# A sparse gate table built by indirect DMA adds in place of one-hot matrix products

## The chip, the cores and the metric

The kernel runs on one core of a Trainium2 chip. That core has five engines with one in-order instruction queue each: TensorE (PE, with PEld for its weight loads), VectorE (DVE), ScalarE (ACT), GpSimd (POOL) and SyncE (SP). SP, ACT and POOL can issue DMA transfers, which 16 shared DMA engines carry out. The metric is the time of one execution in microseconds (us) on the device; lower is better. The kernel before takes 4821.69 us, the median of three runs (4821.6 to 4826.84).

## What is computed

One transformer layer on 512 tokens of width 2048 in float32: a mixer (mLSTM and forgetting attention), a cross attention to a memory of 256 rows, and a PEER feed-forward, each with a residual and a layer norm. The change lies in the last:

```python
def peer_ffn(x, w_pq, sub_keys, expert_u, expert_v):
    q = (x @ w_pq).reshape(B, S, PEER_HEADS, 2, PEER_DK // 2)
    sc = einsum('bshpd,hpnd->bshpn', q, sub_keys)
    top_s, top_i = lax.top_k(sc, 16)                        # on each of two sides, of 128 keys
    cand_s = top_s[..., 0, :, None] + top_s[..., 1, None, :]    # 16 x 16 candidates
    cand_i = top_i[..., 0, :, None] * 128 + top_i[..., 1, None, :]
    best_s, best_pos = lax.top_k(cand_s, 16)
    idx = take_along_axis(cand_i, best_pos)                 # 8 heads x 16 experts a token
    g = softmax(best_s)
    a = einsum('tkd,td->tk', expert_u[idx], x)
    hact = gelu(a) * g
    return einsum('tk,tkd->td', hact, expert_v[idx])
```

There are 128 x 128 = 16,384 experts. Each token picks 16 in each of 8 heads. Two heads of a token may pick the same expert; their gates then add up.

## The kernel before

All large products are run as three float32r products, of a high and a low part of each operand. Weights come in 512 KB pieces on SP's queue (`load_raw`). For each, ACT makes the high part `whi` (line 133) and DVE the low part `wlo` (line 134, a tensor_tensor of two SBUF inputs); this pair is called the split. `work["last"]` holds the last split, and `after(i, other)` makes instruction `i` wait for another; it paces work that is put in between.

The tokens are cut into four blocks of 128. Block 0 (path A) runs ahead of the other three (path B). Early in the kernel, block 0's merge and tail are woven with block B's mLSTM heads (`weave`, line 1127).

The PEER part treats tokens in two ways. 232 of them, block 0 and the last 104 of block 3, are *gathered*: for each of a token's picks, POOL issues an indirect DMA (`gather_rows`, line 917) that fetches 128 expert rows of 8 KB, one a partition, into the three-deep buffer `rows`. DVE then makes the dot product (line 947), or adds the row (line 950). The other `NDENSE = 280` tokens (blocks 1, 2 and 24 tokens of block 3) are *dense*: every expert is computed for them, and a gate table, zero almost everywhere, picks out the few that count.

The dense part has two stages. `stage_a(c)` takes one chunk of 128 experts: 48 matmuls, then a gelu on ACT into `ga` (line 1307). The first `LOOK = 88` chunks run ahead and store `ga` to HBM (`gad`). Then `stage_o` runs in 16 blocks of eight chunks. For each chunk `stage_h` loads the gates `G` (line 1318, four chunks at a time) and `ga`, multiplies them (line 1324) and splits them into `hph` and `hpl`; the matmuls into `po` follow. The remaining 40 chunks of `stage_a` run within these blocks. The rows of the gathered tokens of block 3, as `jobs`, are spread over both stages, `EARLY = 66` of them in the first.

The gates come from `topk` (lines 1218 to 1244): for each block, `select` finds `i0`, `i1` (the two key numbers) and `g` (the score) of the 128 picks of each token, and `soften` makes gates of the scores. `rows_of` copies block 3's picks on POOL into `eid` and `egg` for the gathers. Then, in the code before, the table is built by products. The three arrays are transposed. For each dense token, DVE makes two one-hot rows, one of `i0` and one of `i1` (line 1269), ACT scales one with the gate (line 1274), and PE multiplies them (line 1275); summed over the 128 picks, this gives the token's 128 x 128 gates. ACT copies them from PSUM into `stage` (line 1278) and sends them to HBM as `gd` (line 1280).

The code is written in one order, but a scheduler decides how the instructions of different parts follow each other on each engine; so the build of the table lies among the chunks of `stage_a`. On POOL, each DMA takes one of eight completion semaphores in turn and waits until the last transfer with that semaphore has landed.

Of the kernel before, what the change touches and what calls it, by code (L numbers as in the profile page):

```python
# [21 lines left out]
P = 128  # L22
# [8 lines left out]
PH, PKEYS, TOPK = 8, 128, 16  # L31
NDENSE = 280
GATHERED = ((64, 64), (32, 32), (24, 8))
GB = 56
NEG = -1.0e30
ALPHA = 2.0 ** 0.25
EPS = 1e-5
# [8 lines left out]
def build(tc, I, out):  # L46
    nc = tc.nc
    with ExitStack() as ctx:
# [25 lines left out]
        def nm(s):  # L74
            cnt[0] += 1
            return f"{s}_{cnt[0]}"
# [50 lines left out]
        ioti = cp.tile([P, P], I32, tag="ioti", name="ioti")  # L127
        nc.gpsimd.iota(ioti, pattern=[[1, P]], base=0, channel_multiplier=0)
        nc.vector.tensor_copy(iota, ioti)


        def split(hi, lo, src):
# [583 lines left out]
        def merge(R, Y, G, cpair, tmp):  # L716

            for g in range(4):
                def ev_b(s, b, g=g):
                    m1, t = tmp(R.n), tmp(R.n)  # L720
                    nc.gpsimd.dma_start(m1, mg[g * 4 + s, :, R.cols])
                    nc.gpsimd.dma_start(t, sgd[g * 4 + s, :, R.cols])
                    nc.vector.tensor_mul(t, t, b[:, :R.n])
                    nc.vector.tensor_add(t, t, m1)
                    G.append(cpair())
                    split(*G[-1], t)

                yield from R.group(I["w_br_fx"][g], Y, ev_b)
# [138 lines left out]
        def soften(tp, g):  # L867

            e = g.rearrange("p (h k) -> p h k", k=16)
            sm = tp.tile([P, 8], F32, tag="sm", bufs=2, name=nm("s"))  # L870
            nc.scalar.activation(e, e, AF.Exp)
            nc.vector.tensor_reduce(out=sm, in_=e, axis=AX.X, op=ALU.add)
            nc.vector.reciprocal(sm, sm)
            nc.vector.tensor_tensor(e, e, sm.unsqueeze(2).to_broadcast([P, 8, 16]), op=ALU.mult)
# [153 lines left out]
        with tc.tile_pool(name="sa", bufs=1, side="right", reuse_waits="tile") as sa:  # L1028
# [95 lines left out]
            mbs = ctx.enter_context(ExitStack())  # L1124
            mb = mbs.enter_context(tc.tile_pool(name="mb", bufs=1, reuse_waits="tile"))
            heads = mlstm(B, mb, dict(ka=2, pre=3, qk=5, v=5, o=3, nM=1, pt=5), hold_d)
            weave(chain(merge(A, YA, GA, ac, at), tail_a()), heads, 0.36)

        gat = ctx.enter_context(tc.tile_pool(name="gat", bufs=1, side="right", reuse_waits="tile"))
        work.update(jobs=gathered(0, 0, P, 0, lambda: work["last"], 2), rate=258 / 305)  # L1130
# [45 lines left out]
        with tc.tile_pool(name="xb", bufs=1, reuse_waits="tile") as xp:  # L1176
# [6 lines left out]
            class Rows(list):  # L1183
# [20 lines left out]


        NC_ = PKEYS
        gd = dp.tile([P, NDENSE // GB, NC_, GB], F32, tag="gd", name="gd")
        gap = ctx.enter_context(tc.tile_pool(name="gap", bufs=1, reuse_waits="tile"))
        E = weights(ctx, "w2", 3, 3, 3)
        gad = dp.tile([NC_, P, NDENSE], F32, tag="gad", name="gad")  # L1210
# [3 lines left out]

        sel = {t: {n: pp.tile([P, P], F32, tag=f"{n}{t}", name=f"sel_{n}{t}") for n in ("i0", "i1", "g")}
               for t in range(1, TB)}

        with tc.tile_pool(name="topk", bufs=1, reuse_waits="tile") as tp:
            scs, QB = {}, []
            for g in query(B, X2, lambda: tp.tile([P, B.n], F32, tag="qT", bufs=6, name=nm("qT")), QB):  # L1220
                if g is None:
                    continue
                g, = g
                keysT = tp.tile([P, 4, P], F32, tag="keysT", bufs=2, name=nm("keysT"))
                nc.sync.dma_start(keysT, I["keysT"][:, 4 * g:4 * g + 4])
                for t in range(TB - 1, 0, -1):
                    bank = sm_bank()
                    for j in range(4):
                        nc.tensor.matmul(bank[:, j * P:(j + 1) * P], QB[g][j][:, (t - 1) * P:t * P],
                                         keysT[:, j, :], start=True, stop=True)  # L1230
                    first = t == TB - 1
                    scs[t, g] = tp.tile([P, 512], F32, tag=f"sc{first}", bufs=2 if first else 8, name=nm("sc"))
                    nc.scalar.copy(scs[t, g], bank)
                    if t == TB - 1:
                        select(tp, sel[t], 2 * g, scs[t, g])
            while work["jobs"] is not None:
                if next(work["jobs"], None) is None:
                    work["jobs"] = None
            soften(tp, sel[TB - 1]["g"])
            rows_of(tp, sel[TB - 1], [(1 + i, r0, n) for i, (r0, n) in enumerate(GATHERED)])  # L1240
            for t in range(1, TB - 1):
                for g in range(4):
                    select(tp, sel[t], 2 * g, scs[t, g])
                soften(tp, sel[t]["g"])

        def o_bank(i=0):
            return BK["pool"].tile([P, 512], F32, tag="mm", bufs=BK["mm"], name=nm("po"))


        gs = ExitStack()  # L1250
        gp = gs.enter_context(tc.tile_pool(name="gbuild", bufs=1, reuse_waits="tile"))
        selT = {n: gp.tile([P, NDENSE], F32, tag=n + "T", name=n + "T") for n in ("i0", "i1", "g")}
        turned = 0
        for hb in range(NDENSE // GB):
            while turned * P < (hb + 1) * GB:
                bank = o_bank()
                n = min(P, NDENSE - turned * P)
                for j, m in enumerate(("i0", "i1", "g")):
                    nc.tensor.transpose(bank[:, j * P:(j + 1) * P], sel[turned + 1][m], ident)
                for j, m in enumerate(("i0", "i1", "g")):  # L1260
                    nc.vector.tensor_copy(selT[m][:, turned * P:turned * P + n], bank[:, j * P:j * P + n])
                turned += 1
            stage = [gp.tile([P, 32, GB], F32, tag="stage", bufs=5, name=nm("stage")) for _ in range(4)]
            for q in range(GB // 4):
                ta = hb * GB + q * 4
                bank = o_bank()
                o0, o1 = (gp.tile([P, 4, P], F32, tag=f"o{k}", bufs=2, name=nm("o")) for k in (0, 1))
                for o, k in ((o0, "i0"), (o1, "i1")):
                    onehot = nc.vector.tensor_tensor(o, iota.unsqueeze(1).to_broadcast([P, 4, P]),
                                                     selT[k][:, ta:ta + 4].unsqueeze(2).to_broadcast([P, 4, P]),  # L1270
                                                     op=ALU.is_equal)
                for u in range(4):
                    c = slice(ta + u, ta + u + 1)
                    nc.scalar.activation(o0[:, u], o0[:, u], AF.Copy, scale=selT["g"][:, c])
                    nc.tensor.matmul(bank[:, u * P:(u + 1) * P], o1[:, u], o0[:, u], start=True, stop=True)
                bv = bank.rearrange("p (t c) -> p c t", t=4)
                for ch in range(4):
                    nc.scalar.copy(stage[ch][:, :, q * 4:q * 4 + 4], bv[:, ch * 32:ch * 32 + 32])
            for ch in range(4):
                nc.scalar.dma_start(gd[:, hb, ch * 32:ch * 32 + 32], stage[ch])  # L1280
        gs.close()
        pre.close()


        mn = ctx.enter_context(tc.tile_pool(name="main", bufs=1, reuse_waits="tile"))
        acc = mn.tile([P, NK, NDENSE], F32, tag="acc", name="acc")

        J = 8
        LOOK = 88
        EARLY = 66  # L1290
        fetched, hs, gates = {}, {}, {}

        rings[:] = [W, E]
# [19 lines left out]
        def stage_h(c):  # L1313

            for f in range(c, min(c + 3, NC_)):
                if f // 4 not in gates:
                    gates[f // 4] = mn.tile([P, NDENSE // GB, 4, GB], F32, tag="G", bufs=2, name=nm("G"))
                    nc.sync.dma_start(gates[f // 4], gd[:, :, f:f + 4])
# [4 lines left out]
            gv = ga.rearrange("p (b t) -> p b t", t=GB)  # L1323
            nc.vector.tensor_mul(gv, gv, gates[c // 4][:, :, c % 4])
            a, b = pair(mn, "hp", [P, NDENSE], 2 * J + 2)
            split(a, b, ga)
            hs[c] = (a, b)
# [137 lines left out]
                    last_rows(0, NT, rest)  # L1465

        njobs, done = sum(2 * n + 1 + REST for _, n in GATHERED), 0
        for a in range(LOOK):
            if a >= LOOK - J:
                work["tie"] = onehot  # L1470
            stage_a(a)
            while done * LOOK < a * EARLY:
                next(jobs, None)
                done += 1
        work["tie"] = None


        room = [4 if c0 < LOOK - J else 10 for c0 in range(0, NC_ - 2 * J, J) for _ in range(2 * J)]
# [91 lines left out]
```

## Time and profile before

The profiled execution took 4818.19 us; its span, from the first instruction to the last, is 4816.5 us.

| what | value |
|---|---|
| median of the runs | 4821.69 us |
| profiled execution, its span | 4818.19 us, 4816.5 us |
| busy share of PE, DVE, ACT, POOL | 97%, 78%, 46%, 21% |
| bytes moved | 1437 MB, 298 GB/s in the mean |
| granted clock of TensorE | 0.986 |
| first chunk of stage_a begins | 3056 us |
| one-hot rows, first and last | 3391.6, 3621.7 us |
| first output product | 3676.8 us |

A busy PE is not PE at its peak, as matmuls are pipelined. In rows of busy time by stage, each engine has its busy microseconds and, in brackets, its instructions; behind them stand the granted clock, the share of the DMA engines and GB/s. In a timeline, a row has its start, its length, and in square brackets the idle time before it and what ended it. A POOL row of a DMA is the time to issue it, not the transfer. A row of DMA issues ends with the median time to landing.

### The profile page before, as it was taken

To read this page: it belongs to the slowest core of one execution; us is meant where nothing else is said; L and a number is where in the kernel's file an instruction comes from. 1 tells how busy PE (TensorE), PEld (TensorE's weight loads), DVE (VectorE), ACT (ScalarE), POOL (GpSimd) and SP (SyncE) were. 2 spreads that over 40 slices of the span, in tenths; PEclk is the share of its full clock that TensorE was granted. 3 is DMA by queue.
4 is the path that set the end of the run, shared out by engine and by line. 5 is a ranking of instruction groups with operands and counts; after the bars stand their busy time and mean duration, and the time that the engine had idled before them with its cause. 6 is when DMAs were issued, how large, how long until landed. Compare 5 with 4: busy or idle time off the path is not lost. (4 is left out here: it accounts for less than half of the span.)

```text
span 4816.5 us, 75407 instructions
## 1 busy us (share of the span) xinstructions
PE 4653.0 (97%) x28717; PEld 4299.9 (89%) x28717; DVE 3764.5 (78%) x5357; ACT 2200.1 (46%) x3375; POOL 988.6 (21%) x948
## 2 busy tenths in 40 slices
PE   7999999999999899999999999999998999999998
PEld 6888888887888899999998778999998999899998
DVE  7776677666699677778778578899876999888876
ACT  6665666555543323343332433444784333333342
POOL 0000111200003332333434121211111112122320
PEclk9999999999999999999999999999999999999999
DMA  7888899865569899988899577599888999998983
GB/s 265 289 291 294 314 331 330 278 220 190 192 200 353 318 358 344 328 311 320 288 340 369 202 263 282 190 341 351 300 291 339 362 359 352 328 345 334 348 303 121
DMA packets 372271, 1437.24 MB, mean 298 GB/s; under 512 B 44767, under 2 KB 96207, under 8 KB 311411
## 3 DMA queue, kind: packets, MB, share of 16 engines
q1 hardware_dynamic: 258457, 825.57, 49.1%
q0 software_dynamic: 95008, 571.45, 31.8%
q10 hardware_dynamic: 18441, 35.40, 2.0%
q8 instruction: 225, 3.69, 0.3%
q14 instruction: 140, 1.14, 0.1%
HBM read 1346.03 MB, written 86.06 MB: 297 GB/s over the span
## 5 line engine op out<-in xcount | busy, mean ns | idle before, releaser
L133 ACT CAST whi<-raw 128x1024 fp32r<-128x1024 f32 x1472 | 1530.1, 1052 | 1807.5 <-PE mm L210 827.0
L134 DVE TENSOR_TENSOR wlo<-raw,whi 128x1024 fp32r<-128x1024 f32 x1472 | 1780.5, 1220 | 680.6 <-ACT whi L133 492.4
L950 DVE SCALAR_TENSOR_TENSOR xacc<-rows,dots,xacc 128x2048 f32<-128x2048 f32 x232 | 544.4, 2347 | 38.3 <-DMA rows<-in_peer_v,eid 36.8
L917 POOL DMA_INDIRECT rows<-in_peer_v,eid x232 | 382.5, 1649 | 922.4 <-DVE wlo L134 435.7
L917 POOL DMA_INDIRECT rows<-in_peer_u,eid x232 | 343.7, 1481 | 1066.4 <-DVE rows L947 449.9
L947 DVE SCALAR_TENSOR_TENSOR rows<-rows,xacc 128x2048 f32<-128x2048 f32 x232 | 529.6, 2284 | 41.7 <-DMA rows<-in_peer_u,eid 40.2
L210 PE MATMUL po<-hph,whi 128*128 128x280 f32 x2048 | 533.2, 295 | 20.8 <-ACT hph L133 14.6
L210 PE MATMUL sm<-Ch,whi 128*128 128x280 f32 x2048 | 544.2, 295 | 5.7 <-ACT whi L133 3.9
L210 PE MATMUL sm<-Cl,whi 128*128 128x280 f32 x2048 | 542.6, 293 | 0.0
L210 PE MATMUL po<-hpl,whi 128*128 128x280 f32 x2048 | 531.5, 293 | 2.4 <-DVE hpl L134 2.2
L210 PE MATMUL mm<-xh,whi 128*128 128x384 f32 x1280 | 435.1, 342 | 6.4 <-ACT whi L133 3.6
L210 PE MATMUL mm<-xl,whi 128*128 128x384 f32 x1280 | 428.9, 337 | 0.0
L210 PEld LDWEIGHTS po<-hph,whi 128*128 128x128 f32 x2048 | 378.5, 189 | 28.3 <-ACT hph L133 19.8
L210 PEld LDWEIGHTS sm<-Ch,whi 128*128 128x128 f32 x2048 | 385.7, 188 | 8.6 <-ACT whi L133 5.0
L210 PEld LDWEIGHTS sm<-Cl,whi 128*128 128x128 f32 x2048 | 387.1, 189 | 0.0
L210 PEld LDWEIGHTS po<-hpl,whi 128*128 128x128 f32 x2048 | 379.5, 189 | 6.0 <-DVE hpl L134 4.0
L210 PE MATMUL po<-hph,wlo 128*128 128x280 f32 x2048 | 345.3, 293 | 11.0 <-DVE wlo L134 11.0
L210 PE MATMUL sm<-Ch,wlo 128*128 128x280 f32 x2048 | 314.2, 294 | 0.2 <-DVE wlo L134 0.2
L210 PEld LDWEIGHTS po<-hph,wlo 128*128 128x128 f32 x2048 | 293.8, 189 | 13.6 <-DVE wlo L134 13.2
L210 PEld LDWEIGHTS sm<-Ch,wlo 128*128 128x128 f32 x2048 | 281.6, 189 | 0.4 <-DVE wlo L134 0.4
L210 PE MATMUL mm<-xh,wlo 128*128 128x384 f32 x1280 | 255.0, 335 | 0.0
L210 PEld LDWEIGHTS mm<-xh,whi 128*128 128x128 f32 x1280 | 241.3, 189 | 13.2 <-issue 4.3
(446 smaller groups left out, 8554.5 us busy)
## 6 DMA issues: line engine op xcount, KB each, us to landing
raw<-in_w_in SPq DMA_DIRECT2D x512, 512.0 KB, 5.1
raw<-in_uT SPq DMA_DIRECT2D x256, 512.0 KB, 5.8
raw<-in_vq SPq DMA_DIRECT2D x256, 512.0 KB, 6.9
raw<-in_w_xkv SPq DMA_DIRECT2D x64, 512.0 KB, 4.7
raw<-in_w_br_ml SPq DMA_DIRECT2D x64, 512.0 KB, 5.5
raw<-in_w_br_fx SPq DMA_DIRECT2D x64, 512.0 KB, 5.8
raw<-in_w_out SPq DMA_DIRECT2D x64, 512.0 KB, 4.5
raw<-in_peer_wq SPq DMA_DIRECT2D x64, 512.0 KB, 4.5
```

What stands on the lines that cost most here:

```text
L133: nc.scalar.copy(hi, src)
L134: return nc.vector.tensor_sub(lo, src, hi.bitcast(F32))
L210: nc.tensor.matmul(o, w if stat else x, x if stat else w, start=k == first and x is xh and not part, stop=k == last and part == 1)
L917: i = nc.gpsimd.indirect_dma_start(out=rows, out_offset=None, in_=I[table], in_offset=bass.IndirectOffsetOnAxis(ap=ei[:, k:k + 1], axis=0))
L947: after(nc.vector.scalar_tensor_tensor(rows, rows, 1.0, xacc, op0=ALU.mult, op1=ALU.mult, accum_out=dots[:, k:k + 1]), last())
L950: after(nc.vector.scalar_tensor_tensor(xacc, rows, dots[:, k:k + 1], xacc, op0=ALU.mult, op1=ALU.add), last())
```

## The change

The table is now an array `gtab` in HBM, in the order partition (`i1`), chunk (`i0`), token. It is filled with zeros by 16 POOL transfers early on, which are woven with block B's mLSTM heads (`zeros`). After the softening of a block, two DVE rows compute the place of each pick in the table (`places`). During the first stage POOL then issues 288 indirect transfers that add 128 gates (96 for block 3) at their places, one pick of each token in each. Block 3's 24 dense tokens are first regrouped by eight small copies into `rix` and `rgx`, so that four picks of each go in one transfer. Within one head a token's 16 picks differ; between heads they can coincide, so a head's transfers wait until the previous head of the same block has landed (`add_head`). A small memset, `table`, waits for all; the loads of `G` wait for it. The one-hot rows, the products and `gd` are gone. `LOOK` is 80 in place of 88, `EARLY` 60 in place of 66, and the gather jobs of the first stage begin after `LEAD = 16` chunks.

```diff
+        gtab = nc.dram_tensor("gtab", (P * PKEYS * NDENSE, 1), F32, kind="Internal").ap()
+        gtv = gtab.rearrange("(p c t) o -> p c (t o)", p=P, c=PKEYS)
+        ZK = 8
+        zeroed = []
+        def zeros(gen, pool):
+            zrow = pool.tile([P, NDENSE], F32, tag="zrow", name="zrow")
+            nc.gpsimd.memset(zrow, 0.0)
+            for x in gen:
+                c = len(zeroed) * ZK
+                if c < PKEYS:
+                    i = nc.gpsimd.dma_start(gtv[:, c:c + ZK], zrow.unsqueeze(1).to_broadcast([P, ZK, NDENSE]))
+                    after(i, work["last"])
+                    zeroed.append(i)
+                yield x
...
-            weave(chain(merge(A, YA, GA, ac, at), tail_a()), heads, 0.36)
+            with tc.tile_pool(name="zr", bufs=1, side="right", reuse_waits="tile") as zr:
+                weave(chain(merge(A, YA, GA, ac, at), tail_a()), zeros(heads, zr), 0.36)
...
+        def places(tp, t):
+            row = tp.tile([P, P], F32, tag="ef", bufs=1, name=nm("row"))
+            ix = place[t] = pp.tile([P, P], I32, tag=f"ix{t}", name=f"ix{t}")
+            nc.vector.tensor_scalar(row, sel[t]["i0"], float(NDENSE), pcol[:, t - 1:t], op0=ALU.mult, op1=ALU.add)
+            nc.vector.scalar_tensor_tensor(ix, sel[t]["i1"], float(PKEYS * NDENSE), row, op0=ALU.mult, op1=ALU.add)
...
+            for j in range(SH):
+                for d, a in ((rix, place[TB - 1]), (rgx, sel[TB - 1]["g"])):
+                    nc.gpsimd.dma_start(d[j * REM:(j + 1) * REM], a.rearrange("p (c j) -> p j c", j=SH)[:REM, j])
...
-        for hb in range(NDENSE // GB):
...
-                for o, k in ((o0, "i0"), (o1, "i1")):
-                    onehot = nc.vector.tensor_tensor(o, iota.unsqueeze(1).to_broadcast([P, 4, P]),
-                                                     selT[k][:, ta:ta + 4].unsqueeze(2).to_broadcast([P, 4, P]),
-                                                     op=ALU.is_equal)
-                for u in range(4):
-                    c = slice(ta + u, ta + u + 1)
-                    nc.scalar.activation(o0[:, u], o0[:, u], AF.Copy, scale=selT["g"][:, c])
-                    nc.tensor.matmul(bank[:, u * P:(u + 1) * P], o1[:, u], o0[:, u], start=True, stop=True)
...
-                nc.scalar.dma_start(gd[:, hb, ch * 32:ch * 32 + 32], stage[ch])
+        def add_head(t, h):
+            n, ix, g, k = (SH * REM, rix, rgx, P // SH // PH) if t == TB - 1 else (P, place[t], sel[t]["g"], P // PH)
+            wait = landed.get(t, zeroed)
+            mine = []
+            for c in range(h * k, h * k + k):
+                i = nc.gpsimd.indirect_dma_start(
+                    out=gtab, out_offset=bass.IndirectOffsetOnAxis(ap=ix[:n, c:c + 1], axis=0),
+                    in_=g[:n, c:c + 1], in_offset=None, compute_op=ALU.add)
+                for w in wait:
+                    after(i, w)
...
+                mine.append(i)
+                yield
+            landed[t] = mine
+        def all_heads():
+            for th in "30 10 31 11 32 12 33 13 34 14 35 15 20 16 21 17 22 36 23 37 24 25 26 27".split():
+                yield from add_head(int(th[0]), int(th[1]))
...
-        LOOK = 88
-        EARLY = 66
+        LOOK = 80
+        EARLY = 60
+        LEAD = 16
...
-                    nc.sync.dma_start(gates[f // 4], gd[:, :, f:f + 4])
+                    after(nc.sync.dma_start(gates[f // 4], gtv[:, f:f + 4]), table)
...
+        adds, nadds, added = all_heads(), P * 2 + P // SH, 0
         for a in range(LOOK):
-            if a >= LOOK - J:
-                work["tie"] = onehot
             stage_a(a)
-            while done * LOOK < a * EARLY:
+            while added * (LOOK - 6) < nadds * (a + 1):
+                next(adds, None)
+                added += 1
+            while done * (LOOK - LEAD) < (a - LEAD) * EARLY:
                 next(jobs, None)
                 done += 1
-        work["tie"] = None
+        run(adds)
+        table = nc.gpsimd.memset(gap.tile([P, 1], F32, tag="table", name="table"), 0.0)
+        for i in (i for m in landed.values() for i in m):
+            after(table, i)
```

More of the change, by code (lines that the diff above doesn't have):

```diff
@@ L33 @@
 GATHERED = ((64, 64), (32, 32), (24, 8))
-GB = 56
 NEG = -1.0e30
@@ L129, in build @@
         nc.vector.tensor_copy(iota, ioti)
+        pcol = cp.tile([P, TB - 1], F32, tag="pcol", name="pcol")
+        pcoli = cp.tile([P, TB - 1], I32, tag="pcoli", name="pcoli")
+        nc.gpsimd.iota(pcoli, pattern=[[P, TB - 1]], base=0, channel_multiplier=1)
+        nc.vector.tensor_copy(pcol, pcoli)
+        gtab = nc.dram_tensor("gtab", (P * PKEYS * NDENSE, 1), F32, kind="Internal").ap()
[12 more added lines that the diff above has]
+                yield x
         def split(hi, lo, src):
@@ L1206, in build @@
         NC_ = PKEYS
-        gd = dp.tile([P, NDENSE // GB, NC_, GB], F32, tag="gd", name="gd")
         gap = ctx.enter_context(tc.tile_pool(name="gap", bufs=1, reuse_waits="tile"))
@@ L1216, in build @@
                for t in range(1, TB)}
+        place = {}
+        def places(tp, t):
[3 more added lines that the diff above has]
+            nc.vector.scalar_tensor_tensor(ix, sel[t]["i1"], float(PKEYS * NDENSE), row, op0=ALU.mult, op1=ALU.add)
+        REM, SH = NDENSE - 2 * P, 4
+        rix, rgx = (pp.tile([P, P // SH], d, tag=n, name=n) for n, d in (("rix", I32), ("rgx", F32)))
         with tc.tile_pool(name="topk", bufs=1, reuse_waits="tile") as tp:
@@ L1239, in build @@
             soften(tp, sel[TB - 1]["g"])
+            places(tp, TB - 1)
+            for j in range(SH):
+                for d, a in ((rix, place[TB - 1]), (rgx, sel[TB - 1]["g"])):
+                    nc.gpsimd.dma_start(d[j * REM:(j + 1) * REM], a.rearrange("p (c j) -> p j c", j=SH)[:REM, j])
             rows_of(tp, sel[TB - 1], [(1 + i, r0, n) for i, (r0, n) in enumerate(GATHERED)])
@@ L1244, in build @@
                 soften(tp, sel[t]["g"])
+                places(tp, t)
         def o_bank(i=0):
             return BK["pool"].tile([P, 512], F32, tag="mm", bufs=BK["mm"], name=nm("po"))
[L1250 to L1253, printed above, removed]
-        for hb in range(NDENSE // GB):
[L1255 to L1267, printed above, removed]
-                for o, k in ((o0, "i0"), (o1, "i1")):
-                    onehot = nc.vector.tensor_tensor(o, iota.unsqueeze(1).to_broadcast([P, 4, P]),
-                                                     selT[k][:, ta:ta + 4].unsqueeze(2).to_broadcast([P, 4, P]),
-                                                     op=ALU.is_equal)
-                for u in range(4):
-                    c = slice(ta + u, ta + u + 1)
-                    nc.scalar.activation(o0[:, u], o0[:, u], AF.Copy, scale=selT["g"][:, c])
[L1275 to L1279, printed above, removed]
-                nc.scalar.dma_start(gd[:, hb, ch * 32:ch * 32 + 32], stage[ch])
@@ L1281, in build @@
[L1281 to L1286, printed above, removed]
+        landed, issued = {}, []
+        def add_head(t, h):
[8 more added lines that the diff above has]
+                    after(i, w)
+                for w in issued:
+                    if w not in wait:
+                        tc.declare_no_dep(i.ins, w.ins, reason="other places of the table")
+                issued.append(i)
+                mine.append(i)
+                yield
+            landed[t] = mine
@@ L1316, in stage_h @@
                 if f // 4 not in gates:
-                    gates[f // 4] = mn.tile([P, NDENSE // GB, 4, GB], F32, tag="G", bufs=2, name=nm("G"))
-                    nc.sync.dma_start(gates[f // 4], gd[:, :, f:f + 4])
+                    gates[f // 4] = mn.tile([P, 4, NDENSE], F32, tag="G", bufs=2, name=nm("G"))
+                    after(nc.sync.dma_start(gates[f // 4], gtv[:, f:f + 4]), table)
                 if f < LOOK and f not in fetched:
@@ L1322, in stage_h @@
             ga = fetched[c]
-            gv = ga.rearrange("p (b t) -> p b t", t=GB)
-            nc.vector.tensor_mul(gv, gv, gates[c // 4][:, :, c % 4])
+            nc.vector.tensor_mul(ga, ga, gates[c // 4][:, c % 4])
             a, b = pair(mn, "hp", [P, NDENSE], 2 * J + 2)
@@ L1467, in build @@
         njobs, done = sum(2 * n + 1 + REST for _, n in GATHERED), 0
+        adds, nadds, added = all_heads(), P * 2 + P // SH, 0
         for a in range(LOOK):
-            if a >= LOOK - J:
-                work["tie"] = onehot
             stage_a(a)
-            while done * LOOK < a * EARLY:
+            while added * (LOOK - 6) < nadds * (a + 1):
+                next(adds, None)
+                added += 1
+            while done * (LOOK - LEAD) < (a - LEAD) * EARLY:
                 next(jobs, None)
                 done += 1
-        work["tie"] = None
+        run(adds)
+        table = nc.gpsimd.memset(gap.tile([P, 1], F32, tag="table", name="table"), 0.0)
+        for i in (i for m in landed.values() for i in m):
+            after(table, i)
+        pre.close()
+        mn = ctx.enter_context(tc.tile_pool(name="main", bufs=1, reuse_waits="tile"))
+        acc = mn.tile([P, NK, NDENSE], F32, tag="acc", name="acc")
         room = [4 if c0 < LOOK - J else 10 for c0 in range(0, NC_ - 2 * J, J) for _ in range(2 * J)]
```

## The prediction

> **What bounds the kernel now.** I read the page's engine table first, then busy time by stage, then the rows of the gate build, and last POOL's and DVE's timelines.
>
> ```profile
> PE 4653.0 (97%) x28717; PEld 4299.9 (89%) x28717; DVE 3764.5 (78%) x5357; ACT 2200.1 (46%) x3375; POOL 988.6 (21%) x948
> ...
> core 0: us, PE busy (x) PEld busy (x) DVE busy (x) ACT busy (x) POOL busy (x), PEclk, DMA share, GB/s
> 866.00:976.00 110.00, 108.24 (x521) 93.25 (x519) 77.65 (x132) 60.31 (x80) 18.21 (x35) 1.00 0.79 260
> 3056.00:3677.00 621.00, 610.84 (x4794) 609.07 (x4795) 549.51 (x1009) 351.65 (x836) 123.52 (x111) 1.00 0.85 309
> 3200.00:3400.00 200.00, 200.00 (x1561) 199.82 (x1559) 192.62 (x359) 84.75 (x112) 34.70 (x28) 1.00 0.95 346
> 3679.00:4222.00 543.00, 512.17 (x3818) 499.11 (x3818) 473.97 (x568) 204.85 (x263) 101.46 (x79) 0.98 0.95 351
> ```
>
> PE is busy 97% of the span, and the change works in a stretch where it never rests: from 3200 to 3400 PE shows 200 of 200 us, DVE 192.6 and the DMA engines 0.95. 1561 matmuls in 200 us make 0.128 us each. POOL is the idle engine, 21% over the span.
>
> ```profile
> L1307 ACT ACTIVATE ga<-sm x128: 378/405/547, 3063.8 to 4738.6; 128x280 f32<-128x280 f32 x128
> L210 PE MATMUL po<-hph,whi x2048: 285/291/600, 3676.8 to 4795.0; 128*128 128x280 f32 x187
> L1318 SPq DMA_DIRECT2D G<-gd x32: 529/530/1409, 3659.7 to 4637.3; - x32
> L1275 PE MATMUL po<-o,o x560: 270/275/377, 3398.6 to 3626.8; 128*128 128x128 f32 x187
> L1269 DVE TENSOR_TENSOR o<-iota,i0T x70: 679/685/694, 3391.6 to 3621.1; 128x512 f32<-128x512 f32 x70
> ...
> L1278 ACT COPY stage<-po x280: 242/284/471, 3399.7 to 3628.5; 128x128 f32<-128x128 f32 x140
> ...
> 3398.61 1.05 PE L1275 MATMUL po<-o,o 128*128 128x128 f32 x8
> 3399.42 0.63 PE L210 MATMUL sm<-Ch,wlo 128*128 128x280 f32 x3
> ```
>
> Call the stretch from 3056, where the first expert chunk runs, to 3676.8, where the first output product runs, the first stage: 621 us for 88 chunks. Its 88 x 48 matmuls at 0.128 take 541 us. The one-hot products are 560 matmuls, and eight of them start 0.81 us before what follows (3398.61 to 3399.42), 0.10 each: 56 us. The remaining 24 us are gaps, nearly all at the turn into the second stage.
>
> **The change part by part.**
>
> *One-hot rows and products go.* 56 us of PE in an unbroken stretch, so 56 us of path. DVE's 140 one-hot rows (0.685 us each, 96 us) and ACT's copies are work beside PE and worth nothing by themselves. The turn's gaps go with them, but the turn has a wait of its own afterwards.
>
> *LOOK 88 to 80.* Eight chunks leave the first stage: 80 x 48 x 0.128 = 491 us, so PE alone would be through at 3547. They return in the second stage, where the 3679 to 4222 row shows the DMA engines at 0.95 and 351 GB/s with PE at 512 of 543. There bytes set the pace. It gets 8 x 1.05 MB of expert rows more, six gathers of 1.05 MB more (EARLY 66 to 60), and eight read-backs of 0.14 MB fewer: 13.6 MB, at 351 GB/s 39 us. The table is read in runs of 4,480 bytes, formerly 896. Between 0 and some 10 us lie there; I take 4. Second stage: +35 us (bounds 25 by those bytes, 49 if the eight chunks cost PE in full).
>
> *Zero fill.* 18.35 MB go out in 16 transfers. In the order of the built program they stand beside transfers that ran at 866 to 976. The row there shows 260 GB/s, 91 below the 351 of the later stretch; in 110 us that leaves room for 10 MB. The other 8 MB would cost 24 us at 351 GB/s if the loads fell behind at once, and nothing if they catch up afterwards. I take 10. Each fill waits on POOL for a DVE split, and the small loads of the merge queue behind it; at one split of 1.2 us a time that is hidden by the same buffers, 16 x 1.2 = 19 us if it were not.
>
> *Small edits.* Two DVE rows a block for the places (under 2 us in all); eight element-wise copies to regroup block 3 on POOL, at most 0.74 us each as the 512-row copy below, 6 us ahead of the eid copies, covered because the first gather is now held to chunk 16.
>
> *The adds.* 288 indirect transfers join POOL's queue. In the built order 32 of block 3 with 8 gathers come first; then 256 of blocks 1 and 2 in 16 heads with 42 gathers between them, three after nearly every head. What does one cost POOL?
>
> ```profile
> 3105.62 0.51 POOL L912 DMA_DIRECT2D egg<-sel_g  x1
> 3106.44 1.01 POOL L917 DMA_INDIRECT rows<-in_peer_u,eid  x1 [0.30 <-issue]
> 3107.75 0.97 POOL L917 DMA_INDIRECT rows<-in_peer_u,eid  x1 [0.30 <-issue]
> ...
> 3145.56 0.95 POOL L917 DMA_INDIRECT rows<-in_peer_u,eid  x1 [3.69 <-DVE rep L827]
> 3149.65 1.69 POOL L917 DMA_INDIRECT rows<-in_peer_u,eid  x1 [3.14 <-DVE rows L947]
> 3167.03 0.94 POOL L917 DMA_INDIRECT rows<-in_peer_u,eid  x1 [4.80 <-DVE v L828]
> 3173.09 1.95 POOL L917 DMA_INDIRECT rows<-in_peer_u,eid  x1 [5.11 <-DVE ix L829]
> 3203.01 0.94 POOL L917 DMA_INDIRECT rows<-in_peer_u,eid  x1 [5.12 <-DVE s L872]
> ...
> 3149.30 1.22 DVE L134 TENSOR_TENSOR wlo<-raw,whi 128x1024 fp32r<-128x1024 f32 x1
> 3166.89 0.66 DVE L861 TENSOR_REDUCE sel_i<-eq 128x32 f32<-128x512 f32 x1
> 3173.02 1.20 DVE L134 TENSOR_TENSOR wlo<-raw,whi 128x1024 fp32r<-128x1024 f32 x1
> ...
> core 0: us, POOL busy (x), PEclk, DMA share, GB/s
> 3105.00:3700.00 595.00, 104.91 (x69) 0.99 0.88 323
> ...
> L436 POOL DMA_DIRECT2D md<-zo x32 | 22.1, 737 | 140.4 <-ACT zo L434 139.6 <-ACT aq L600 0.8
> ...
> rows<-in_peer_u,eid POOLq DMA_INDIRECT x64, 8.6
> egg<-sel_g POOLq DMA_DIRECT2D x16, 0.2 KB, 3.2
> ```
>
> A direct copy takes POOL 0.51 us. An indirect gather takes 0.94 at best, with 0.30 of issue between two of them: 1.24 apart. And it is stretched by DVE. The gather at 3149.65 fell into a split of two SBUF inputs (3149.30 to 3150.43, when the next instruction starts) and ended 0.91 us after it; so did the one at 3173.09. The one at 3167.03 fell beside a reduction with one input and took 0.94. Over 3105 to 3700 the mean is 104.91 / 69 = 1.52, so 0.58 of contention and, with the issue gap, 1.82 apart. The low end for an add is the direct 0.51. I take the indirect row, since an add reads its places from SBUF as a gather does and names as many rows. Contention scales with DVE's duty: 19 POOL operations a head over a stage stretched from 350 to some 500 us leave 0.58 x 350 / 500 = 0.4, rounded down to 0.36 because splits stop when DVE waits. So 1.6 us each.
>
> The Trainium skill, page SBUF — State Buffer, section Who interferes with whom, lets a DVE instruction with two SBUF inputs contend with a GpSimd instruction that reads SBUF, but reports its own probe in which tensor_tensor did not stall a DMA issued from GpSimd. By that probe an add would cost 1.24; the rows at 3149.65 and 3173.09 say otherwise for indirect transfers, and the sum goes by them.
>
> Next, the waits. A head waits until the same block's previous head has landed: 3.2 us by the small copy, 8.6 by the gather, against three gathers of some 1.6 us in between: 0 to 3.8, I take 1.5, times 16 = 24 us. The Trainium skill, DMA: Bandwidth & Descriptors, section Anatomy of one DMA — SWDGE, gives 2.0 us plus the bytes' time; by it these 24 us would be nothing, but the 0.2 KB copy's 3.2 us is the measured price.
>
> Block 1's gates are softened at about 3203 (the gather there was released by L872). The 40 operations before fill the time from 3113 (the gather at 3106.44 plus the regrouping copies): 40 x 1.6 = 64, plus seven waits of some 4, is 3205. From there 298 operations x 1.6 = 477, plus 24: the last add is down at 3706. Then come the table mark, the gate load and the first output product; that chain took 3676.8 - 3659.7 = 17 us, so 3723. That is 46 us later than now, in place of 3547 + 17 = 3564. PE doesn't run ahead meanwhile: the gathers stand behind the adds in POOL's order, DVE's dot products wait for the gathers, and the splits that PE needs stand behind them on DVE. SP's weight loads in turn stand behind the first gate load.
>
> Sum, against the profiled execution (4818.19 us, span 4816.5; the median of the runs is 4821.69, 0.07% above): 46 + 35 + 10 = +91, **4909 us**.
>
> **The rivals.**
>
> *POOL keeps pace (other side).* If adds come no more than 1.15 us apart ((3547 - 3205) / 298), PE sets the end: 3564 - 3677 + 45 = -68, 4750 us. It decides at (3632 - 17 - 24 - 3205) / 298 = 1.30. For it: four bytes a row may take less than 8 KB. Against: the best gap in the trace is 1.24 with no contention at all.
>
> *DVE doesn't hold the adds.* 298 x 1.24 = 370, down at 3599 with the waits, product at 3616: -61 + 45 = -16, 4802 us. For it: the back-to-back gathers at 3106 and 3107 ran unstretched. Against: those at 3149 and 3173. The probe on the Trainium skill's page SBUF — State Buffer would bring this case about.
>
> *Landing sets the pace.* POOL's transfers take turns on eight completion marks, so a head of 16 needs two landings. Above 12.8 us (half of 16 x 1.6) these bind; at twice the gather's 8.6 a head takes 34 us and its gathers 4, 16 x 38 = 613, product at 3835: +158 + 45 = +203, 5021 us. For it: adds queue behind three 1 MB gathers, and each reads and rewrites HBM, which no row here prices. Against: small copies land in 3.2.
>
> *It cancels*: adds at 1.30 to 1.38, within 10 us of 4818.
>
> **How the numbers follow.** Forecast 0.56; POOL keeps pace 0.15; DVE doesn't hold 0.10; cancels 0.05; landing 0.14. 0.2% (10 us) is about what a measurement of this kernel can tell. Faster is 0.15 + 0.10 = 0.25, same 0.05, slower 0.70. The range goes from 4760, within the keeps-pace case, to 5021. The forecast's own range, with adds at 1.4 to 1.85 us and the two other terms at their bounds, is 4830 to 5010.
>
> **What would show it.** The one-hot rows and L1275's products are gone and the first product comes near 3723; adds show 0.94 with stretches to a split's end; POOL is above 85% busy in the first stage with DVE waiting there for gathers; PE falls below 7 matmuls a us before the turn; the second stage is about 35 us longer. A first product near 3565 with POOL pausing for DVE's splits would make it wrong, as would adds well under 0.9 us.

## The result and the profile after

The changed kernel takes 5042.74 us, the median of four runs (5037.21 to 5046.81), beside 4821.66 for the kernel before on the same chip. The ratio is 1.0455, with a 95% interval of 1.0437 to 1.0473: 4.5% slower, 221 us. The forecast was 4909 and the range ended at 5021. The sign was right, the size was two and a half times too small, and the time lies outside the range.

The page's table of engines has PE at 92% where it was at 97%, and POOL at 30% instead of 21%:

```profile
PE 4636.4 (92%) x28148; PEld 4275.8 (85%) x28148; DVE 3678.1 (73%) x5215; ACT 2076.0 (41%) x2814; POOL 1520.6 (30%) x1263
```

Three views show where the time lies: the rows of the tiles `ga`, `gtab` and `hph` of the changed kernel (shortest, median and longest instruction in ns, first and last start in us) ...

```profile
L1336 ACT ACTIVATE ga<-sm x128: 383/404/413, 3081.0 to 4967.4; 128x280 f32<-128x280 f32 x128
...
L1297 POOL DMA_INDIRECT gtab<-sel_g,ix x256: 1537/1544/3661, 3234.5 to 3843.2; - x128
L1297 POOL DMA_INDIRECT gtab<-rgx,rix x32: 1412/1564/5209, 3133.4 to 3228.2; - x32
...
L230 PE MATMUL po<-hph,whi x2048: 285/292/601, 3861.9 to 5023.9; 128*128 128x280 f32 x187
```

... busy time by stretch, the second row over just the adds of blocks 1 and 2 ...

```profile
core 0: us, PE busy (x) PEld busy (x) DVE busy (x) ACT busy (x) POOL busy (x), PEclk, DMA share, GB/s
3080.00:3234.00 154.00, 148.75 (x1138) 148.53 (x1137) 137.85 (x397) 65.53 (x78) 100.74 (x92) 0.98 0.76 222
3234.00:3850.00 616.00, 375.98 (x2654) 372.09 (x2652) 271.58 (x381) 140.93 (x170) 522.96 (x303) 0.80 0.70 188
3850.00:4120.00 270.00, 245.41 (x1815) 241.98 (x1816) 239.87 (x283) 100.14 (x134) 61.60 (x44) 0.95 0.98 372
```

... and the longest waits between 3150 and 3900 (total, times, longest):

```profile
DVE rows L967 <- DMA rows<-in_peer_u,eid: 343.8, 21, 36.0
...
PEld sm L230 <- DVE wlo L154: 193.7, 17, 26.8
PE sm L230 <- DVE wlo L154: 189.9, 17, 26.6
POOL gtab L1297 <- issue: 87.3, 276, 3.6
...
PE po L230 <- ACT hph L153: 70.4, 2, 67.3
```

Before, PE was busy in every microsecond from 3200 to 3400. Now it works 376 of 616 us. POOL is busy for 523 of these 616 us, with 303 instructions (256 adds, 46 gathers and the memset `table`); at 0.30 us of issue between two of them, 91 more, that is all of its time. Behind POOL the line of waits is as the prediction drew it: DVE's dot product waits for a gather that stands behind adds (344 us), and PE waits for the split that stands behind the dot product on DVE (190 us). So PE's last chunk of the stage ends only at 3794.6. Then PE waits 67 us more, for the first `hph`, which needs the table; the last add starts at 3843.2.

The 228.6 us between the two spans split at two marks. The first `ga` starts 17.2 us later (3081.0 against 3063.8). The first output product starts 185.1 us later (3861.9 against 3676.8), so 167.9 arise in the first stage. From there to the end it takes 1183.2 us against 1139.7, 43.5 more.

### The profile page after: what moved, and what is told of

Read it like the earlier page. It is cut to its first block, busy times and chain, and to the rows that moved or that the text cites. A ratio compares the mean times of both kernels' runs of the same rounds, so it can differ in the third digit from the quotient of the medians.

```text
span 5045.1 us, 73707 instructions
## 1 busy us (share of the span) xinstructions
PE 4636.4 (92%) x28148; PEld 4275.8 (85%) x28148; DVE 3678.1 (73%) x5215; ACT 2076.0 (41%) x2814; POOL 1520.6 (30%) x1263
## 5 line engine op out<-in xcount | busy, mean ns | idle before, releaser
L937 POOL DMA_INDIRECT rows<-in_peer_u,eid x232 | 310.7, 1339 | 680.9 <-DVE rows L967 384.9
L1297 POOL DMA_INDIRECT gtab<-sel_g,ix x256 | 479.1, 1871 | 78.0 <-issue 76.8
L230 PEld LDWEIGHTS sm<-Ch,whi 128*128 128x128 f32 x2048 | 398.0, 194 | 3.9 <-ACT xacc L991 3.2
L230 PEld LDWEIGHTS sm<-Cl,whi 128*128 128x128 f32 x2048 | 397.3, 194 | 0.0
```

What stands on the lines that cost most here:

```text
L230: nc.tensor.matmul(o, w if stat else x, x if stat else w, start=k == first and x is xh and not part, stop=k == last and part == 1)
L937: i = nc.gpsimd.indirect_dma_start(out=rows, out_offset=None, in_=I[table], in_offset=bass.IndirectOffsetOnAxis(ap=ei[:, k:k + 1], axis=0))
L1297: i = nc.gpsimd.indirect_dma_start(out=gtab, out_offset=bass.IndirectOffsetOnAxis(ap=ix[:n, c:c + 1], axis=0), in_=g[:n, c:c + 1], in_offs ...
```

## The experiments

**Is it the adds? All of them left out.**

```diff
-            for th in "30 10 31 11 32 12 33 13 34 14 35 15 20 16 21 17 22 36 23 37 24 25 26 27".split():
+            for th in "".split():
...
-        adds, nadds, added = all_heads(), P * 2 + P // SH, 0
+        adds, nadds, added = all_heads(), 0, 0
```

> The changed kernel with all 288 adds left out (the table stays zero, so block gates 1 to 3 are zero); zero fill, places, gathers, chunk counts and read-back stay. Theory, the adds alone make the loss: 80 chunks at 6.14 us from 3082 and 17 of turn, first product near 3590, second stage 1183 as measured with the adds, time near 4775, below the kernel before. Rival, the gathers held to chunk 16 and then set closer (0.9 a chunk against 0.75) hold PE by themselves: first product 3640 or later, time 4825 or more.

Measured: 4746.04 us, ratio 0.9844 (0.9827 to 0.986). The row of `hph` in this kernel, and its busy time over the stretch of the adds:

```profile
L230 PE MATMUL po<-hph,whi x2048: 285/291/435, 3575.7 to 4725.0; 128*128 128x280 f32 x187
```

```profile
3234.00:3850.00 616.00, 602.05 (x4611) 597.49 (x4609) 526.28 (x681) 243.34 (x313) 137.89 (x91) 0.99 0.95 357
```

The first product comes at 3575.7, where the prediction had put PE's own end with the turn and the zero fill (3547 + 17 + 10 = 3574). That agreement is in part luck. The first `ga` starts 18.7 us later than before (3082.5), not 10, PE takes 10 us more than the 491 for its chunks, and the 17 us of the turn do not arise: the product starts as the last matmul of `stage_a` ends. The rival, that the denser gathers hold PE, falls: PE is busy 602 of the 616 us in which it was busy 376. The rest of the change is a gain of 74 us, and the 288 adds cost 5042.7 - 4746.0 = 297.

**What makes an add dear? Plain writes in place of adds.**

```diff
-                    in_=g[:n, c:c + 1], in_offset=None, compute_op=ALU.add)
+                    in_=g[:n, c:c + 1], in_offset=None)
```

> The adds are turned into plain indirect writes (the addition is left out, so gates of picks that fall on one place are overwritten); count, order, waits and bytes stay. Theory A, the accumulation is what makes an add's best time 1.54 us where a gather's is 0.94: the best time falls to about 0.94, 256 adds save 0.6 us each, 154 us, the first output product comes near 3862 - 154 = 3708 and the time is near 4890. Theory B, a scatter into HBM (or its one-element rows) costs it, whatever is done there: the best time stays at 1.54, first product 3862, time 5040. Theory C, the landing of a head sets the pace: best time may fall, POOL then waits, time within 20 us of 5040.

Measured: 4927.99 us, ratio 1.0216 (1.0193 to 1.024); first product at 3742.9. The rows of `gtab` in this kernel, then its costliest group of them (busy us, mean ns; idle time and what ended it):

```profile
L1297 POOL DMA_INDIRECT gtab<-sel_g,ix x256: 965/991/3100, 3230.3 to 3725.0; - x128
L1297 POOL DMA_INDIRECT gtab<-rgx,rix x32: 904/930/4520, 3139.8 to 3226.5; - x32
```

```profile
L1297 POOL DMA_INDIRECT gtab<-sel_g,ix x256 | 364.0, 1422 | 78.0 <-issue 75.3 <-DMA gtab<-sel_g,ix 2.7
```

The same group in the changed kernel:

```profile
L1297 POOL DMA_INDIRECT gtab<-sel_g,ix x256 | 479.1, 1871 | 78.0 <-issue 76.8 <-DMA gtab<-sel_g,ix 1.2
```

Theory A holds: an indirect write without the addition costs POOL 0.965 us at best, within 0.03 of a gather; with it, 1.537. The addition adds 0.57 us of POOL time to each transfer. Theory B (scatter or one-element rows) falls, and so does C: POOL waited 2.7 us in all for landings. The first product came 119 us earlier and not 154, as the mean fell by 0.45 only. The stretch above the best time grew from 0.33 to 0.46: PE got on faster, and more of DVE's work fell beside POOL's instructions (154 of the 256 transfers met a DVE instruction of two inputs, where 120 of the adds did). So of the 297 us the addition makes 115 and the transfers as such 182.

**Is PE held through the gathers? No gather in the first stage.**

```diff
-        EARLY = 60
+        EARLY = 0
```

> No gather of block 3 in the first stage (EARLY 0), all adds stay there. Theory, PE was held by the order add, gather, dot product, split: now PE runs the 80 chunks unheld and is through near 3575, POOL needs 256 adds of 2.0 us from 3217, about 3760, PE rests for some 190 us, and the first product comes near 3775. The second stage takes the 50 gathers, 1.05 MB each, 150 us more at 351 GB/s: time near 5110. Rival, the adds themselves (their writes, their contention with DVE) slow PE's work: PE goes through its chunks no faster than with the gathers, its last chunk near 3800, as in the changed kernel.

Measured: 5154.41 us, ratio 1.0701 (1.0674 to 1.0729); first product at 3795.9. Busy time by stretch:

```profile
3234.00:3450.00 216.00, 216.00 (x1678) 216.00 (x1677) 103.72 (x142) 89.37 (x109) 178.69 (x101) 1.00 0.83 194
...
3550.00:3720.00 170.00, 0.00 (x0) 0.00 (x0) 0.00 (x0) 0.00 (x0) 136.14 (x89) 0.50 0.23 0
```

With all adds in place and no gather among them, PE is busy 216 of 216 us. So at this spacing neither the adds' writes nor their contention slows PE. As gathers without adds did not hold it either (the first experiment), it takes both: the gathers pass POOL's lateness on. PE stopped earlier than expected, near 3513, because on ACT's in-order queue a cast of `hph` stood ahead of weight casts for the last of the 80 chunks, and waited 243 us for loads that came only when the table was done. The second row measures the adds alone, beside a DVE that does nothing: 89 in 170 us, 1.91 apart, waits included.

**Does half of the adds cost half? Block 2's left out.**

```diff
-            for th in "30 10 31 11 32 12 33 13 34 14 35 15 20 16 21 17 22 36 23 37 24 25 26 27".split():
+            for th in "30 10 31 11 32 12 33 13 34 14 35 15 16 17 36 37".split():
...
-        adds, nadds, added = all_heads(), P * 2 + P // SH, 0
+        adds, nadds, added = all_heads(), P + P // SH, 0
```

> Block 2's 128 adds are left out (its gates stay zero in the table); the gathers stay. Theory POOL: 128 x 2.17 us = 278 fewer on POOL, so POOL no longer ends last; the first output product falls to about 3600, where PE's own 491 us after 3081 and the turn put it, and the time to about 4781. Rival, the small writes slow the DMA engines, and with them loads and gathers: half the writes give half of the 168 us back, first product near 3778, time near 4960. Rival, the wait for a head's landing: block 1's heads now follow each other with only their three gathers between, waits grow from 10 us in all to some 8 x 5 = 40, time near 4820.

Measured: 4899.94 us, ratio 1.0157 (1.0134 to 1.0181); first product at 3721.5. None of the three forecasts fits. The table was ready long before the first output product:

```profile
L1297 POOL DMA_INDIRECT gtab<-sel_g,ix x128: 1537/1548/4895, 3238.7 to 3549.7; - x128
...
L1347 SPq DMA_DIRECT2D G<-gtab x32: 320/346/1039, 3555.2 to 4720.9; - x32
```

I had taken the later of POOL's end and PE's own end. But while the adds ran, PE got through fewer chunks, and afterwards it could only go at its own pace. Each chunk leaves one `ga`; this kernel's count of them by stretch (ACT busy us, count):

```profile
3234.00:3350.00 116.00, 4.86 (x12) 0.84 0.74 198
3350.00:3450.00 100.00, 3.24 (x8) 0.80 0.74 196
3450.00:3550.00 100.00, 4.46 (x11) 0.86 0.69 185
3550.00:3650.00 100.00, 5.22 (x13) 0.95 0.99 391
```

31 chunks in 316 us, which at 6.14 us a chunk (48 x 0.128) is 190 us of work: 126 us lost, for good. Another 21 go in one wait behind the adds: SP's queue, with the weights, stands from 3534.7 to 3555.2 at the first load of `G`, which waits for the table, and a cast of weights on ACT then stands 20.9 us, until 3569.3. 3575.7 + 126 + 21 = 3723, against 3721.5 measured.

**Can more of PE's work cover the adds? All 128 chunks ahead.**

```diff
-        LOOK = 80
-        EARLY = 60
+        LOOK = 128
+        EARLY = 100
```

> All 128 chunks in the first stage (LOOK 128) and EARLY 100 in place of 60: 128 x 6.14 = 786 us of PE from 3081, so POOL's 288 adds and some 85 gathers, at 2.04 each 760 us less what lies before 3217, end near 3217 + 650 = 3870 to 3930. Theory POOL: first product near 3910; the second stage loses 48 chunks and 35 gathers, 85 MB or 240 us at 351 GB/s, though PE keeps 834 us of it: 3910 + 870 to 950, time 4780 to 4860. Rival, what the adds cost is not POOL time that PE's work can cover: the first stage grows with the chunks by 48 x 7.7 = 370 and the second falls by 240, time near 5170.

Measured: 5029.34 us, ratio 1.0429 (1.0406 to 1.0451); first product at 4122.5. Between the two forecasts. The adds still ran from 3239.4 to 3845.8, and PE got 62 chunks done in the 612 us from 3234: 381 us of work, 231 lost. Here too one wait follows: a cast of weights stands 26.1 us for the first load of `G`. From the first `ga` at 3085.8, 127 x 6.14 + 231 + 26 gives 4123. The longer first stage bought only 13 us, because the adds did not spread over it: 256 of them ran beside these 62 chunks, about 4 a chunk, and none beside the 43 that followed.

**Does their density matter? Each add held to the newest split.**

```diff
                 for w in wait:
                     after(i, w)
+                after(i, work["last"])
```

Run with LOOK 128 and EARLY 100, with EARLY 60, with block 2's adds left out, and with the change's own LOOK 80:

> As look128 (128 chunks in the first stage, EARLY 100), but every add is also held to the newest DVE split, so that in the built order 2 to 3 adds and one gather stand at each chunk instead of 4.4 adds a chunk up to chunk 79 and none after. Theory: PE loses time only where the adds stand denser than POOL can issue them in a chunk's 6.14 us; now 2.64 adds and 0.89 gathers a chunk at 2.04 us are 7.2 us from 3239 on, 97 chunks end at 3938, first product near 3955, second stage 905 as in look128, time near 4860. Rival: an add costs PE the same wherever it stands (235 us of loss over 256 adds in look128, 0.92 each): first product stays near 4122, time near 5030.

> As tied, with EARLY 60: 2.64 adds and 0.55 gathers a chunk, 6.5 us, so PE's 6.14 are nearly kept: first product near 3890; the second stage gets some 33 gathers more than in tied, 100 us at 351 GB/s: 905 + 100 = 1005, time near 4895. Rival as in tied: first product near 4115, time near 5100.

> As half (block 2's adds left out, LOOK 80, EARLY 60), with the adds held to the newest split: 2.2 adds and 0.9 gathers a chunk, 6.2 us of POOL. Theory of density: PE keeps nearly its pace, first product 3600 to 3650 in place of 3722, time near 4800. Rival, 0.95 us of PE for each add wherever it stands: first product 3722, time 4900.

> The changed kernel with its own LOOK 80 and EARLY 60, every add also held to the newest DVE split. Theory, with 80 chunks POOL's total binds and not how the adds stand: 298 operations of 2.04 or more from 3217, first product 3860 to 3900, time 5040 to 5080. Rival, density alone: first product earlier by some 50 to 80 us as in tied, time near 4970.

| held to the split | time us | ratio | first product | not held |
|---|---|---|---|---|
| LOOK 128, EARLY 100 | 4950.15 | 1.0267 (1.025 to 1.0285) | 4043.6 | 5029.34, 4122.5 |
| LOOK 128, EARLY 60 | 4989.43 | 1.0356 (1.0332 to 1.0379) | 3973.0 | not run |
| half the adds, LOOK 80 | 4850.37 | 1.0054 (1.0036 to 1.0072) | 3681.5 | 4899.94, 3721.5 |
| LOOK 80, EARLY 60 | 5048.89 | 1.0472 (1.0455 to 1.049) | 3863.3 | 5042.74, 3861.9 |

Density counts where POOL isn't the last to end: the first product comes 79 us earlier with 128 chunks and 40 earlier with half the adds. It counts for nothing at 80 chunks, where POOL ends last; that forecast was met. In the other three rows the first product came between the two forecasts (3955 and 4122 for the first row), so density explains part of the loss and not all of it. Busy time of the first row's kernel:

```profile
3234.00:4000.00 766.00, 625.95 (x4569) 616.38 (x4568) 451.63 (x501) 235.03 (x291) 655.06 (x353) 0.92 0.87 264
```

POOL has no time left here either: 655 us and 353 gaps of 0.30 are 761 of 766. 353 operations in 766 us are 2.17 apart, where I had counted 342 at 2.04, 698 us. A faster PE brings more DVE work beside POOL (DVE is busy 452 of 766 us, 59%, against 272 of 616, 44%), and each add grows: 1.998 us in the mean, against 1.871.

**What do the small parts cost? The zero fill alone, and the chunk counts alone.** The first puts `zeros` and its weave into the kernel before; the second is

```diff
-        LOOK = 88
-        EARLY = 66
+        LOOK = 80
+        EARLY = 60
```

in the kernel before.

> The kernel before with the zero fill of the table alone (18.35 MB in 16 transfers on POOL's queue, tied as in the change; nothing reads the table). If the fill makes the 17 us by which the first expert chunk came later: time near 4837. If those came from another edit: near 4821.

> The kernel before with LOOK 80 and EARLY 60 in place of 88 and 66, nothing else. Theory, the second stage's 43 us come from the eight chunks and six steps moved there: first product at 3677 - 49 = 3628, second stage 1140 + 35 to 44, time 4802 to 4811. Rival, they come from the table's read-back and layout: second stage grows by under 20 us, time near 4785.

The fill alone: 4831.87 us against 4824.33, ratio 1.0016 (1.0006 to 1.0026). Its first `ga` starts at 3073.7, 10 us later than before. The other 7 of the 17 are not explained by it. In the ten profiled kernels that share the change's code up to there, the first `ga` starts between 3074.6 and 3087.1, so a single profile can't tell 7 us.

The chunk counts alone: 4846.31 us, ratio 1.0054 (1.0038 to 1.0071). The first product comes at 3649.9, 27 us earlier and not 49, since the one-hot work doesn't shrink with the chunks; PE was busy 123.92 of the last 140 us before 3590, and waited 14.2 us for ACT's scaled one-hot rows, where it was 4.9 before. The second stage takes 4840.6 - 3649.9 = 1190.7, 51 us more than before, so the time missed both forecasts, 4802 to 4811 and 4785. Without any adds (the first experiment) the second stage takes 4746.2 - 3575.7 = 1170.5, 31 more, though it reads the new table. So the 43.5 come from the moved chunks and gathers, and the table's read-back costs nothing that these runs show.

No version run here that holds all the adds is faster than the kernel before. The change without adds gains 74 us; the cheapest complete form, held to the split with 128 chunks, is 4950 - 4746 = 204 us above that, though that comparison mixes 128 chunks with 80, as no run without adds had 128.

## Why the prediction was wrong

| step | predicted | measured |
|---|---|---|
| zero fill, before the first stage | +10 | +17 (fill alone: +10) |
| block 1's adds begin | 3205 | 3234.5; 3217 without those 17 |
| POOL time of an add, undisturbed | 0.94 | **1.54** |
| issue gap | 0.30 | 0.30 |
| stretch by DVE, per add | 0.36 | 0.33 |
| waits for the landing of blocks 1 and 2's heads | 24 | 1.2 |
| end of the last add on POOL to first product | 17 | 17.2 |
| second stage | +35 | +43.5 |
| no adds: first product | 3574, fill included | 3575.7 |

**The step that failed is the price of an add.** "I take the indirect row, since an add reads its places from SBUF as a gather does and names as many rows." That holds for the indirect write: 0.965. It leaves out the addition, 0.57 us of POOL's own time, of which no row of the trace before could say anything. The only bounds set there were 0.51 below and "1.4 to 1.85 us" apart for the forecast's own range; measured from the first add of block 1 to the end of the last add were 298 operations, as counted, in 610 us, 2.05 apart with the cheaper gathers among them, and 1.87 + 0.30 = 2.17 for an add. On 256 adds, 0.60 more is 154 us. Against it stand 23 us less of landing waits, 8 of contention (256 x 0.03), and 14 from the 42 gathers between, which POOL issued in 0.97 and 0.30 rather than at the flat 1.6. The later start adds 12: together 121, where the first product missed by 122, the zero fill apart (3845 against 3723).

A cost above the indirect row belonged in the range: the add had one more thing to do than any row showed, and a row that is "nearest" to an unseen operation is a lower bound for it when the unseen one does everything the row does and more. With plain writes, the same sum would have come out right in its total: first product 3723 + 17 = 3740 by the prediction's spacing of 1.6, measured 3742.9. Its terms would not: the writes took 1.42 + 0.30 = 1.72 each, and shorter waits and cheaper gathers made up for it.

**The mechanism was right.** POOL's in-order queue became the bound of the first stage; gathers stood behind adds, dot products behind gathers, splits behind dot products. PE fell to 2654 / 616 = 4.3 matmuls a us, where "below 7" had been named as the sign. That it is the gathers which keep PE from running ahead was shown by the run without early gathers. SP's loads stood behind the first gate load, as predicted, for 21 us with half the adds and 26 with 128 chunks. That PE is held also meant more than the prediction drew from it: for the end of the stage I compared POOL's end with PE's, and the half and the 128-chunk run showed that PE's lost chunks add up instead. Two slips did not matter: the 24 us of gaps "nearly all at the turn" are not in the row shown, where PE is idle for 10 of 621 us, and 16 x 38 is 608 and not 613.

**The stretch by DVE was sized right,** 0.33 against 0.36. Timeline rows of the changed kernel show it, two adds beside an idle DVE and one beside a dot product and a split:

```profile
3499.34 1.54 POOL L1297 DMA_INDIRECT gtab<-sel_g,ix  x1 [0.30 <-issue]
3501.18 1.54 POOL L1297 DMA_INDIRECT gtab<-sel_g,ix  x1 [0.30 <-issue]
3503.02 1.00 POOL L937 DMA_INDIRECT rows<-in_peer_u,eid  x1 [0.30 <-issue]
...
3510.63 1.86 POOL L1297 DMA_INDIRECT gtab<-sel_g,ix  x1 [0.30 <-issue]
...
3508.78 2.29 DVE L967 SCALAR_TENSOR_TENSOR rows<-rows,xacc 128x2048 f32<-128x2048 f32 x1 [21.10 <-DMA rows<-in_peer_u,eid]
3511.00 1.21 DVE L154 TENSOR_TENSOR wlo<-raw,whi 128x1024 fp32r<-128x1024 f32 x1
```

Of the 256 adds, the 135 that ran beside no DVE instruction took 1.55 us in the mean and 1.61 at most; the 120 that met one with two inputs took 2.24 in the mean.

The Trainium skill, page SBUF — State Buffer, section Who interferes with whom, gives both the rule that a DVE instruction with two SBUF inputs contends with a GpSimd instruction that reads SBUF, and a probe in which tensor_tensor did not hold up a DMA issued from GpSimd. These runs stand with the rule. So does the run without early gathers: 89 adds of 136.14 us, 1.53 each, while DVE did nothing, and 178.69 / 101 = 1.77 while DVE was busy 48% of the time.

**Of the rivals,** "POOL keeps pace" and "DVE doesn't hold the adds" needed adds 1.15 and 1.24 apart; the 128-place adds of the changed kernel never came closer than 1.84. "Landing sets the pace" named 5021, near the measured time, but for a reason that isn't there: POOL's adds waited 9.7 us for landings, 8.5 for block 3's and 1.2 for the others'. The chain that ended last has the last add's landing:

```profile
3843.20 2.96 DMA gtab<-sel_g,ix
```

It landed 2.96 us after its issue began, and the three gathers between two heads of a block (3 x 1.27 us) covered that. By the 2.0 us plus bytes of the Trainium skill, page DMA: Bandwidth & Descriptors, section Anatomy of one DMA — SWDGE, these waits would have been nothing, which is nearer to the measurement than my 24; the landing itself, 2.96 us from the start of the issue, took longer than that 2.0. In the run without early gathers the adds of blocks 1 and 2 waited 17 us for such landings.

**The second stage** was put at +35, between 25 and 49; the changed kernel's 43.5 lies between them, and the six other kernels with LOOK 80 and EARLY 60 show between +31 and +51.

**What stays open:** what POOL does in the 0.57 us of the addition; 7 us ahead of the first stage; and whether fewer or cheaper adds (the picks of one place summed beforehand) could bring the cost under the 74 us that the change otherwise gains, which wasn't tried.

## What to carry to other kernels

An engine that is 21% busy on average may still become the bound of the stage that gets the work: multiply the instructions by their issue-to-issue distance in that stage, and not by their best time. Price a kind of transfer that the trace doesn't hold from the nearest row upward, as far as it does something more than that row; here one operand of the call was worth 115 us. And where an in-order engine feeds the pacing engine, lost time adds up over the stretch in which it is late: spreading that work helps only while the engine has time left, and giving the pacing engine more to do in the stage won back only 13 of 221 us here, 93 with the work spread over it as well.

## What was not expected of the hardware

An accumulating indirect transfer of 128 four-byte values costs POOL 1.537 us at best, a plain one 0.965. With 96 places they cost 1.412 and 0.904, so about 4 and 2 ns a place, and most of the price is fixed. While only adds ran, the DMA engines were 23% busy moving next to no bytes (0 GB/s by the row at 3550): 0.23 x 16 x 170 / 89 = 7 us of engine time for each add. And the clock granted to TensorE was 0.80 over the 616 us in which PE kept stopping, and 0.50 while it rested, against 0.99 in the same stretch without adds. At the clock of 0.80 PE's busy time was 375.98 / 2654 = 0.142 us a matmul, against 602.05 / 4611 = 0.131 at 0.99.
